# Planned slack ahead of the transposes of softmax and 1/rms, and the output projections in three parts instead of two

## The chip, the cores and the metric

The kernel runs on one core of one Trainium2 chip. The time is that of the device for one execution, in microseconds (us); "the median" is that of three executions. One further execution was recorded by the hardware profiler; all durations and waits below are from it. TensorE multiplies matrices (PE in the profile, its weight loads PEld), VectorE (DVE) and ScalarE (ACT) work element by element, GpSimd (POOL) computes a few small powers, and the queue of SyncE (SP) starts the transfers between HBM and the on-chip memory SBUF. TensorE writes its results to banks of the accumulator memory PSUM.

## What is computed

Two layers of a decoder over 256 positions of width 1024, all in float32. Each layer normalizes x, projects it to 4360 columns, runs three groups of heads, and adds an output projection of their joint result to x:

```python
def hybrid_layer(x, norm_w, w_in, ..., w_out):
    h = rmsnorm(x, norm_w)
    proj = jnp.matmul(h, w_in)
    (aq, ak, av, ag, bq, bk, bv, bg, cq, ck, cv, co, cg, ci, cf) = jnp.split(proj, cuts, axis=-1)
    ya = merge_heads(moba_attention(aq, ak, av)) * silu(ag)      # 8 heads, softmax with a distance term
    yb = head_norm(retention(rotate(bq), rotate(bk), bv)) * silu(bg)   # 4 heads
    yc = head_norm(mlstm(conv(cq, ck), cv, ci, cf) * sigmoid(co)) * silu(cg)   # 4 heads
    return x + jnp.matmul(jnp.concatenate([ya, yb, yc], -1), w_out)

def reference(x, ...):
    for layer in range(2):
        x = hybrid_layer(x, ...)
    return rmsnorm(x, final_norm_w)
```

With 256 positions and blocks of 256, the block-sparse attention is plain causal attention with a distance term.

## The kernel before

x lies transposed in SBUF (`px`), so that the projections need no transposes of it. Weights come in chunks of up to 128x2112 through three `raw` buffers. Each chunk is split into two parts, `hi` (rounded by ScalarE to float32r, the type of the matmuls) and `lo` (what is left, subtracted by VectorE), with three buffers each; x is split in the same way into `xh` and `xl` (the tile `xx`), the heads' result y into `yh` and `yl`. A product is then three matmuls: hi*hi, hi*lo, lo*hi. Projections accumulate in four PSUM banks `pj`; everything else that TensorE makes (scores, transposes, attention times values) goes to four banks `mx`. A chunk's `hi` and `lo` buffers are given back once the last matmul that reads them has been placed.

The order of the instructions on every engine is set when the program is built, by the class `Sched`. Each step of work is a generator that yields one instruction at a time with an engine and an estimated cost. The scheduler keeps a planned time for each engine, and always places next the instruction that can start earliest by that plan; among equals a priority decides. An instruction of a thread may start when its own predecessor is planned to end, plus 230 ns (`LAT`) if that was on another engine. `wait(ev)` holds a thread until an event's planned time. What is placed is final: at run time each engine takes its instructions in that order and waits by semaphores where an operand isn't there. The plan's costs decide the order and nothing else.

The three places that the change touches are these. `norm(l)` computes 1/rms: sums of squares, a power on GpSimd (`G(630, ...)`, line 488), and then two transposes on TensorE (`TR`, line 285) that spread it over a row, `rrow`. The queries and keys of all groups are scaled by it. `head_a` is one head of the softmax: scores (`dots`), a maximum by VectorE into `sb`, two exponentials by ScalarE on `sb`, and three transposes of `sb` into a bank `pt`, which ScalarE copies to `et`; `pair_a` then multiplies `et` by the values `va`. The output projections are the last part of `project` for the first layer and `out_last` for the second. Both take four weight chunks (`ws_`, rows 768, 512, 0 and 256 of w_out) in two parts of two: for each PSUM bank the matmuls of both chunks of the part, then the next bank; the buffers of both come back after the last bank. In the first layer a part waits at its start for the first half of each of its chunks.

Two more helpers matter here. `evac_gate` makes the gate tiles `t` (one for each half of the positions) from the last projections, multiplies them by the heads' results `hc`, `on_b` or `on_a` on VectorE, and `y_out` transposes them on TensorE into `mx`. `head_norm` normalizes heads on VectorE, with a power on GpSimd (line 1095). In the records all VectorE work has line 259, all ScalarE work 265, matmuls 280, transposes 285 and transfers 288, because helpers issue them.

Of the kernel before, what the change touches and what calls it, by code (L numbers as in the profile page):

```python
# [12 lines left out]
AF = mybir.ActivationFunctionType  # L13
# [215 lines left out]
def trunk(ctx: ExitStack, tc: tile.TileContext, xp: bass.AP, w: bass.AP, fn: bass.AP,  # L229
# [41 lines left out]
    def G(cost, fn, after=None):  # L271
        return op("pool", cost, fn, after)
# [17 lines left out]
    def wait(ev):  # L290
        return ("wait", ev)
# [4 lines left out]
    def acq(tag):  # L296
        return ("acq", tag)


    px = sb_tile([128, P_N + KT * S], "px")  # L300
# [166 lines left out]
    def norm(l):  # L467
# [19 lines left out]
        rs = tiny(2)  # L487
        yield G(630, lambda: nc.gpsimd.tensor_tensor(rs, ms, mhalf[:, :2], op=OP.pow))  # L488
        yield wait(E("tab"))
        for b in range(2):  # L490
            yield TR(p[:, 128 + b * 128:256 + b * 128], rs[:, b:b + 1].to_broadcast([128, 128]))
# [69 lines left out]
    def project():  # L561
        for l in range(DEPTH):
# [103 lines left out]

            for part in (ws_[:2], ws_[2:]):
                at_chunk[0] = part[-1][0]
                if part[0] is ws_[2]:
                    sc.spawn(norm(l + 1), -1)  # L670
                for i, _ in part:
                    yield wait(E("w", i, 0))
                for ds_, tag in groups:
# [24 lines left out]
    def out_last(base):  # L698
# [3 lines left out]
        acc = {}  # L702
        for part in (0, 1):
            pw = ws_[2 * part:2 * part + 2]
            at_chunk[0] = pw[-1][0]
            for b in range(2):
# [3 lines left out]
                for j, (c0, c1) in enumerate(cuts):  # L710
                    if part == 0:
                        acc[b, c0] = yield acq("mx" if c0 == 768 else "pj")
# [3 lines left out]
                    for n, (i, ch) in enumerate(pw):  # L716
                        h = his[i][:, :2048].rearrange("p (r c) -> p r c", r=2)
                        lo = los[i][:, :2048].rearrange("p (r c) -> p r c", r=2)
                        for r in range(2):
                            yield wait(E("w", i, r))  # L720
                            yield wait(E("y", l, ch + r))
                            yield M(o, yh[:, ch + r, bs], h[:, r, c0:c1], part + n + r == 0, False)
                            yield M(o, yh[:, ch + r, bs], lo[:, r, c0:c1], False, False)
                            e = yield M(o, yl[:, ch + r, bs], h[:, r, c0:c1], False, part + n + r == 3)
# [126 lines left out]
    def head_a(l, g, u, hh, et, done):  # L851
# [12 lines left out]
        yield A(sb[:, 0:128], sb[:, 0:128], AF.Exp, scale=f, bias=m[:, 0:1])  # L864
        yield A(sb[:, 128:384], sb[:, 128:384], AF.Exp, scale=f, bias=m[:, 1:2])
        pt = yield acq("mx")
        for j in range(3):
            e = yield TR(pt[:, j * 128:(j + 1) * 128], sb[:, j * 128:(j + 1) * 128])
# [336 lines left out]
```

## Time and profile before

| | |
|---|---|
| median of three executions | 303.66 us (303.3 to 306.15) |
| the profiled execution | 304.55 us |
| its span, from the first instruction to the last | 302.8 us |
| TensorE busy | 293.0 us (97%), 1792 records |
| VectorE busy | 259.4 us (86%) |
| ScalarE busy | 195.2 us (64%) |
| GpSimd busy | 16.7 us (6%) |
| transfers' share of 16 DMA engines | 45.8% |
| share of the chain that ended last | PE 82%, ACT 9% |
| granted TensorE clock, mean | 0.997 |

The profiled execution took 1.75 us more than its span and 0.89 us more than the median. "Busy" is a sum over the whole program and hides stages; matmul ends are modelled, so that waits on TensorE are read from the distance between starts.

### The profile page before, as it was taken

The numbers are of one execution on the slowest core, as the hardware profiler recorded it, in microseconds if no ns is written. First come the engines' busy times: TensorE is split into PE (matmuls) and PEld (weight loads), VectorE is DVE, ScalarE is ACT, GpSimd is POOL, SyncE is SP. The second block draws the span as 40 slices with busy tenths as digits, with TensorE's granted clock in tenths as the row PEclk, the third lists the DMA queues.
The fourth block names the chain that finished last, engine by engine and source line by source line (L and its number), as shares of the span: only waits on it lengthen the run. The fifth ranks groups of instructions, "written<-read, shape, count | busy, mean of one in ns | idle before, by whom it ended". The sixth has DMA issues, their size and how long they took to land.

```text
span 302.8 us, 4794 instructions
## 1 busy us (share of the span) xinstructions
PE 293.0 (97%) x1792; PEld 258.7 (85%) x1792; DVE 259.4 (86%) x551; ACT 195.2 (64%) x339; POOL 16.7 (6%) x19
## 2 busy tenths in 40 slices
PE   8899999999999999999999999999999999999991
PEld 6798989888999888899988888988899988888881
DVE  3878999989999999766879999999999999867553
ACT  5966999699537528635666689778645264944332
POOL 5001000000002002000020000000002003000010
PEclk9999999999999999999999999999999999999998
DMA  6999446555610434841616751646540625250003
GB/s 199 378 384 359 143 153 227 192 203 197 218 63 0 149 130 139 278 141 19 261 16 259 245 181 41 238 141 202 215 141 0 218 77 179 84 210 0 0 2 139
DMA packets 9095, 48.58 MB, mean 160 GB/s; under 512 B 1008, under 2 KB 1904, under 8 KB 4080
## 3 DMA queue, kind: packets, MB, share of 16 engines
q1 hardware_dynamic: 9072, 48.28, 45.8%
q8 instruction: 14, 0.23, 0.3%
q14 instruction: 9, 0.07, 0.1%
HBM read 47.23 MB, written 1.05 MB: 159 GB/s over the span
## 4 chain that ended last, share of the span: by engine, by line
PE 82%; ACT 9%; issue 2%; DMA 2%; POOL 1%; DVE 1%; SPq 1%; POOLq 0%
PE pj L280 64%; PE mx L280 14%; ACT t L265 4%; PE mx L285 4%; ACT hi L265 3%; DMA px<-xp 2%; POOL small L488 1%; DVE lo L259 1%; ACT sb L265 1%; SPq L288 1%; ACT st L265 1%; POOL small L547 0%; ACT xx L265 0%; ACT raw L265 0%; POOLq L1201 0%
## 5 line engine op out<-in xcount | busy, mean ns | idle before, releaser
L259 DVE TENSOR_TENSOR lo<-raw,hi 128x1024 fp32r<-128x1024 f32 (+2 forms) x96 | 102.8, 1085 | 8.7 <-ACT hi L265 8.6
L280 PE MATMUL pj<-hi,xx 128*128 128x512 f32 (+1 forms) x320 | 93.1, 372 | 0.0
L265 ACT ACTIVATE hi<-raw 128x1024 fp32r<-128x1024 f32 (+2 forms) x96 | 88.4, 946 | 6.6 <-DMA raw<-w 3.3
L280 PE MATMUL pj<-xx,hi 128*128 128x512 f32 (+1 forms) x272 | 88.0, 377 | 0.8 <-ACT hi L265 0.8
L280 PE MATMUL pj<-xx,lo 128*128 128x256 f32 x240 | 69.2, 288 | 0.3 <-DVE lo L259 0.2
L280 PEld LDWEIGHTS pj<-hi,xx 128*128 128x128 f32 x320 | 57.5, 188 | 9.1
L280 PE MATMUL pj<-lo,xx 128*128 128x512 f32 (+1 forms) x160 | 59.7, 373 | 0.0
L280 PEld LDWEIGHTS pj<-xx,hi 128*128 128x128 f32 x272 | 50.1, 193 | 10.1 <-ACT hi L265 1.9
L280 PEld LDWEIGHTS pj<-xx,lo 128*128 128x128 f32 x240 | 45.9, 191 | 0.8 <-DVE lo L259 0.7
L280 PEld LDWEIGHTS pj<-lo,xx 128*128 128x128 f32 x160 | 30.1, 188 | 4.5
L265 ACT ACTIVATE t<-pj 128x256 f32<-128x256 f32 x26 | 9.8, 378 | 18.4 <-PE pj L280 18.4
L265 ACT ACTIVATE sb<-sb,small 128x128 f32<-128x128 f32 (+1 forms) x48 | 19.3, 447 | 3.2 <-DVE sb L259 2.1
L265 ACT ACTIVATE st<-t 64x512 fp32r<-64x512 f32 x26 | 16.1, 627 | 5.8 <-DVE small L259 3.2
L1095 POOL TENSOR_TENSOR small<-small,mhalf 128x8 f32<-128x8 f32 x4 | 7.5, 1868 | 181.6 <-DVE small L259 181.6
L280 PE MATMUL pj<-yh,lo 128*128 128x256 f32 x56 | 16.0, 286 | 0.0
L280 PE MATMUL pj<-yh,hi 128*128 128x256 f32 x56 | 15.9, 284 | 0.0
L280 PE MATMUL pj<-yl,hi 128*128 128x256 f32 x56 | 15.8, 283 | 0.0
L280 PE MATMUL mx<-st,st 128*128 128x128 f32 (+1 forms) x64 | 15.0, 269 | 0.0
L265 ACT ACTIVATE t<-pj,small 128x512 f32<-128x512 f32 (+1 forms) x12 | 7.3, 610 | 9.2 <-PE pj L280 9.2
L265 ACT ACTIVATE t<-t 32x512 f32<-32x512 f32 (+1 forms) x20 | 12.5, 629 | 0.3
L280 PEld LDWEIGHTS mx<-st,st 128*128 128x128 f32 x64 | 12.1, 189 | 0.4
L259 DVE TENSOR_TENSOR t<-pj,t 128x256 f32<-128x256 f32 x26 | 10.9, 418 | 1.8 <-ACT t L265 1.5
(151 smaller groups left out, 481.5 us busy)
## 6 DMA issues: line engine op xcount, KB each, us to landing
raw<-w SPq DMA_DIRECT2D x37, 1024.0 KB, 4.8
raw<-w SPq DMA_DIRECT2D x2, 1056.0 KB, 5.4
raw<-w SPq DMA_DIRECT2D x6, 256.0 KB, 5.4
raw<-w SPq DMA_DIRECT2D x2, 512.0 KB, 6.2
tb<-tab SPq DMA_DIRECT2D x1, 960.0 KB, 9.7
px<-xp SPq DMA_DIRECT2D x3, 256.0 KB, 5.2
tb<-tab SPq DMA_DIRECT2D x1, 514.0 KB, 7.1
raw<-w SPq DMA_DIRECT2D x4, 128.0 KB, 2.9
```

What stands on the lines that cost most here:

```text
L259: return op("dve", cost, lambda: getattr(nc.vector, name)(out, *a, **k), after)
L265: return op("act", cost, lambda: nc.scalar.activation(out, in_, func, **k), after)
L280: return op("pe", cost, lambda: nc.tensor.matmul(out, a, b, start=start, stop=stop, skip_group_check=True), after)
L285: return op("pe", 110.0, lambda: nc.tensor.transpose(out, in_, idn))
L288: return op("sp", cost, lambda: nc.sync.dma_start(out, in_))
L488: yield G(630, lambda: nc.gpsimd.tensor_tensor(rs, ms, mhalf[:, :2], op=OP.pow))
L1095: yield G(1600, lambda: nc.gpsimd.tensor_tensor(vs, vs, mhalf[:, :8], op=OP.pow))
```

## The change

A new helper `pause(t)` holds a thread until the planned time t. In `norm` the two transposes of 1/rms now start, by the plan, no earlier than 500 ns after the end of the power as other engines see it (the value that `yield` gives back, the end plus 230 ns); in `head_a` the three transposes no earlier than 400 ns after that of the second exponential, with the bank `pt` taken ahead of the pause. No instruction is added for this: other work that is ready takes the place in between. The output projections of both layers now go over the banks three times: with the first chunk, with the second, and with the third and fourth together. In the first layer the wait at a part's start for all its chunks is gone (each matmul still waits for its own half). The number of matmuls and the flags of first and last accumulation are the same in effect.

```diff
+    def pause(t):
+
+        ev = Event()
+        ev.time = t
+        return wait(ev)
...
-        yield G(630, lambda: nc.gpsimd.tensor_tensor(rs, ms, mhalf[:, :2], op=OP.pow))
+        e = yield G(630, lambda: nc.gpsimd.tensor_tensor(rs, ms, mhalf[:, :2], op=OP.pow))
         yield wait(E("tab"))
+        yield pause(e + 500)
         for b in range(2):
             yield TR(p[:, 128 + b * 128:256 + b * 128], rs[:, b:b + 1].to_broadcast([128, 128]))
...
-            for part in (ws_[:2], ws_[2:]):
+            for part in (ws_[:1], ws_[1:2], ws_[2:]):
                 at_chunk[0] = part[-1][0]
                 if part[0] is ws_[2]:
                     sc.spawn(norm(l + 1), -1)
-                for i, _ in part:
-                    yield wait(E("w", i, 0))
                 for ds_, tag in groups:
...
-        for part in (0, 1):
-            pw = ws_[2 * part:2 * part + 2]
+        for pw in (ws_[:1], ws_[1:2], ws_[2:]):
+            part = len(pw) - 1
             at_chunk[0] = pw[-1][0]
...
-                    if part == 0:
+                    if pw[0] is ws_[0]:
                         acc[b, c0] = yield acq("mx" if c0 == 768 else "pj")
...
-                            yield M(o, yh[:, ch + r, bs], h[:, r, c0:c1], part + n + r == 0, False)
+                            yield M(o, yh[:, ch + r, bs], h[:, r, c0:c1], pw[0] is ws_[0] and r == 0, False)
                             yield M(o, yh[:, ch + r, bs], lo[:, r, c0:c1], False, False)
                             e = yield M(o, yl[:, ch + r, bs], h[:, r, c0:c1], False, part + n + r == 3)
...
-        yield A(sb[:, 128:384], sb[:, 128:384], AF.Exp, scale=f, bias=m[:, 1:2])
+        e = yield A(sb[:, 128:384], sb[:, 128:384], AF.Exp, scale=f, bias=m[:, 1:2])
         pt = yield acq("mx")
+        yield pause(e + 400)
         for j in range(3):
             e = yield TR(pt[:, j * 128:(j + 1) * 128], sb[:, j * 128:(j + 1) * 128])
```

Because every later choice of the scheduler depends on the earlier ones, instructions move all over the program. Transfers and GpSimd keep their order, and two copies of x for the last sum move from VectorE to ScalarE. Three places follow.

On TensorE, in the first layer, at the transposes of 1/rms (`small` is the tile of small values; `pj_120` and `pj_121` are the banks of the projection that runs meanwhile, `xx` the split x, `hi_90` and `lo_93` the weights):

```order
 L280 MATMUL pj_121<-xx,lo_93 128x256
 L280 MATMUL pj_120<-xx,hi_90 128x512
+L280 MATMUL pj_120<-xx,lo_93 128x256
+L280 MATMUL pj_121<-xx,hi_90 128x512
+L280 MATMUL pj_121<-xx,lo_93 128x256
 L285 MATMUL mx_122<-tb,small 128x128 x2
-L280 MATMUL pj_120<-xx,lo_93 128x256
-L280 MATMUL pj_121<-xx,hi_90 128x512
-L280 MATMUL pj_121<-xx,lo_93 128x256
```

Three matmuls of the projection now stand ahead of the two transposes. At the first softmax of each layer the transposes of `sb` move back in the same way.

On TensorE, in the second layer, where the second four heads' softmax meets the first gates (`t` are gate tiles, `sb_111` to `sb_113` the heads' exponentials). Before:

```order
L280 MATMUL pj_120<-hi_88,xx 128x512
L280 MATMUL pj_121<-hi_88,xx 128x512
L285 MATMUL mx_123<-tb,sb_111 128x128 x3
L280 MATMUL pj_121<-lo_91,xx 128x512
L280 MATMUL pj_121<-hi_88,xx 128x512
L285 MATMUL mx_125<-tb,sb_112 128x128 x3
L280 MATMUL pj_120<-hi_88,xx 128x512
L285 MATMUL mx_122<-tb,t_95 128x128
L285 MATMUL mx_122<-tb,t_97 128x128
```

The same place now:

```order
L280 MATMUL pj_120<-hi_88,xx 128x512
L280 MATMUL pj_121<-hi_88,xx 128x512
L285 MATMUL mx_122<-tb,t_99 128x128
L285 MATMUL mx_122<-tb,t_97 128x128
L285 MATMUL mx_122<-tb,t_99 128x128
L285 MATMUL mx_122<-tb,t_97 128x128
L285 MATMUL mx_125<-tb,sb_111 128x128 x3
L285 MATMUL mx_124<-tb,sb_112 128x128 x3
L280 MATMUL pj_121<-lo_91,xx 128x512
```

The four gate transposes, which stood behind those of two heads and three matmuls, now stand ahead of all of these.

On VectorE, in the same stretch, somewhat earlier (`zu` and `zd` are the rests of the split keys, `small` 128x8 are the sums of `head_norm`, whose power GpSimd takes between the TENSOR_SCALAR and the later TENSOR_TENSOR on it; ISA is the maximum of a head's scores). Before:

```order
L259 TENSOR_TENSOR zu_108<-t_96,st_100 64x512
L259 TENSOR_REDUCE small<-t_99 128x8
L259 TENSOR_TENSOR zd_110<-t_96,st_101 64x512
L259 TENSOR_SCALAR small<-small 128x8
L259 TENSOR_TENSOR lo_92<-raw_86,hi_89 128x1024
L259 ISA sb_111,small<-mx_123,tb 128x128
L259 ISA small 128x1
L259 TENSOR_TENSOR lo_92<-raw_86,hi_89 128x1024
L259 TENSOR_TENSOR small<-small 128x8
```

The same place now:

```order
L259 TENSOR_TENSOR lo_92<-raw_86,hi_89 128x1024
L259 TENSOR_REDUCE small<-t_96 128x8
L259 CAST st_101<-t_94 64x512
L259 TENSOR_SCALAR small<-small 128x8
L259 TENSOR_TENSOR zu_108<-t_94,st_100 64x512
L259 TENSOR_TENSOR zd_110<-t_94,st_101 64x512
L259 TENSOR_TENSOR lo_92<-raw_86,hi_89 128x1024
L259 TENSOR_TENSOR small<-small 128x8
L259 ISA sb_111,small<-mx_125,tb 128x128
```

The first of the maxima comes after both halves of `lo` and after the product with the power, and between the power's input and its use stand three instructions that read two SBUF tiles each.

## Rows read from the trace of the kernel before

**Rows 1.** The page's first part: busy us (share of span) xinstructions.

```profile
PE 293.0 (97%) x1792; PEld 258.7 (85%) x1792; DVE 259.4 (86%) x551; ACT 195.2 (64%) x339; POOL 16.7 (6%) x19
```

**Rows 2.** Timeline of PE at both transposes of 1/rms: start, duration, what [idle before].

```profile
23.00 0.39 PE L280 MATMUL pj<-xx,hi 128*128 128x512 f32 x1
23.62 0.43 PE L285 MATMUL mx<-tb,small 128*128 128x128 f32 x2 [0.23 <-POOL small L488]
...
157.75 0.27 PE L280 MATMUL pj<-xx,lo 128*128 128x256 f32 x1
158.12 0.43 PE L285 MATMUL mx<-tb,small 128*128 128x128 f32 x2
```

**Rows 3.** Timeline of PE at four heads' softmax transposes.

```profile
43.77 0.27 PE L285 MATMUL mx<-tb,sb 128*128 128x128 f32 x1
...
44.54 0.48 PE L280 MATMUL pj<-xx,hi 128*128 128x512 f32 x1
...
181.31 0.78 PE L285 MATMUL mx<-tb,sb 128*128 128x128 f32 x3
181.85 0.36 PE L280 MATMUL pj<-xx,lo 128*128 128x256 f32 x1
...
185.53 0.40 PE L280 MATMUL pj<-xx,hi 128*128 128x512 f32 x1
185.76 0.27 PE L285 MATMUL mx<-tb,sb 128*128 128x128 f32 x1
...
186.64 0.36 PE L280 MATMUL pj<-xx,lo 128*128 128x256 f32 x1
...
259.11 0.49 PE L285 MATMUL mx<-tb,sb 128*128 128x128 f32 x3
259.35 0.48 PE L280 MATMUL pj<-lo,xx 128*128 128x512 f32 x1
```

**Rows 4.** Timeline of PE in both output projections.

```profile
141.83 0.28 PE L280 MATMUL pj<-yh,hi 128*128 128x256 f32 x1
141.95 0.28 PE L280 MATMUL pj<-yl,hi 128*128 128x256 f32 x1
142.22 0.39 PE L280 MATMUL pj<-yh,lo 128*128 128x256 f32 x1
...
287.06 0.40 PE L280 MATMUL pj<-hi,yh 128*128 128x512 f32 x1
287.61 0.50 PE L280 MATMUL pj<-lo,yh 128*128 128x512 f32 x1
287.95 0.40 PE L280 MATMUL pj<-hi,yl 128*128 128x512 f32 x1
```

**Rows 5.** Stretch 159 to 260.5: length, busy PE, PEld, DVE, ACT, POOL; PEclk; DMA.

```profile
159.00:260.50 101.50, 101.02 (x598) 88.42 (x597) 98.39 (x215) 67.61 (x113) 4.18 (x2) 1.00 0.48 166
```

**Rows 6.** Timeline of VectorE: its two real gaps from 159 to 229 us.

```profile
177.60 0.42 DVE L259 TENSOR_TENSOR t<-pj,t 128x256 f32<-128x256 f32 x1 [0.58 <-ACT t L265]
...
213.31 1.23 DVE L259 TENSOR_TENSOR lo<-raw,hi 128x1024 fp32r<-128x1024 f32 x1 [0.41 <-ACT hi L265]
```

**Rows 7.** Timeline of weight loads near 229 us.

```profile
229.19 0.19 PEld L280 LDWEIGHTS mx<-ub,sel 128*128 128x128 f32 x1 [0.22 <-DVE on_a L259]
```

**Rows 8.** Timeline of VectorE, second layer, ahead of the gates' transposes.

```profile
252.22 1.22 DVE L259 TENSOR_TENSOR lo<-raw,hi 128x1024 fp32r<-128x1024 f32 x1
...
254.97 0.17 DVE L259 TENSOR_TENSOR small<-small 128x8 f32<-128x8 f32 x1 [0.18 <-POOL small L1095]
...
259.14 0.75 DVE L259 TENSOR_TENSOR t<-t,hc 128x256 f32<-128x256 f32 x2
```

**Rows 9.** Timeline of PE at the gates' first transposes.

```profile
260.46 0.49 PE L285 MATMUL mx<-tb,t 128*128 128x128 f32 x3
```

**Rows 10.** Timeline of GpSimd: both powers of the second layer's `head_norm`.

```profile
230.82 1.64 POOL L1095 TENSOR_TENSOR small<-small,mhalf 128x8 f32<-128x8 f32 x1 [72.75 <-DVE small L259]
252.39 2.54 POOL L1095 TENSOR_TENSOR small<-small,mhalf 128x8 f32<-128x8 f32 x1 [19.93 <-DVE small L259]
```

## The prediction

> **What bounds the kernel now.** I read the page's busy times first, then the distances between starts on TensorE, then what ended each distance that is longer than usual, and last how full the other engines are in the stretches where that happens. TensorE is busy 293.0 of 302.8 us and VectorE 259.4 [rows 1]. So a transpose that stands too early in TensorE's order holds up the matmuls behind it, and those set the end. What such a wait costs is the distance from one start to the next less what the same pair usually takes: 0.12 us behind a matmul of 256 columns (141.83 to 141.95) [rows 4], 0.23 us behind one of 512 (185.53 to 185.76) [rows 3], and 0.24 us from the first of three transposes to the matmul behind them (259.11 to 259.35) [rows 3].
>
> The second thing to see is that TensorE isn't alone. From 159 to 260.5 us, which is most of the second layer, VectorE is busy 98.39 of 101.50 us [rows 5]. Its two real gaps there before 229 us are 0.58 us at 177, for a copy by ScalarE, and 0.41 us at 213, for a weight half that ScalarE hadn't rounded yet [rows 6]. Near 229 us TensorE waits 0.22 us for a bank that VectorE has just emptied [rows 7]. Here both engines run side by side, and time taken off one alone is not time off the kernel.
>
> **The change part by part.**
>
> The transposes of 1/rms. In the first layer the start comes 0.62 us after that of the matmul of 512 columns ahead of it [rows 2], 0.39 us more than usual; in the second 0.37 us after one of 256 columns, 0.25 us more. The order now puts three matmuls ahead of the first pair (256, 512 and 256 columns: 0.12 + 0.23 + 0.12 = 0.47 us), which covers 0.39; in the second layer the same kind of step covers 0.25. Both waits go, 0.64 us. What is late next is the copy to `rrow` and all that is scaled by it; the pair itself comes 0.1 to 0.3 us later than now, which VectorE takes up in the second layer in its gap of 0.58 us [rows 6], so I cost that at nothing; without that cover it would cost those 0.1 to 0.3 us.
>
> The softmax transposes. Three heads wait: 43.77 to 44.54 is 0.77 us against 0.24, so 0.53; 181.31 to 181.85 gives 0.54 - 0.24 = 0.30; 185.76 to 186.64 gives 0.88 - 0.24 = 0.64 [rows 3]. Together 1.47 us. All other heads have their exponentials in time, and for them the pause buys nothing. The 400 ns are planned time, and ScalarE lies behind its plan when it is crowded, but the matmuls put ahead (three in the first layer, 0.58 us; more in the second) are longer than the waits of 0.53 and 0.30, and about as long as that of 0.64. I take all of it as gone from these places. The price is that `et`, and so attention times values, comes later by as much; those products have other matmuls ahead of them in the order and nobody else queued behind, so nothing is added.
>
> The output projections. The third and fourth chunks' halves could only be split once both earlier chunks were given back. The waits for `lo` are 0.27 - 0.12 = 0.15 us at 141.95, and 0.55 - 0.23 = 0.32 plus 0.34 - 0.23 = 0.11 for the matmul behind it at 287.06 [rows 4]. With the first chunk taken singly its buffers come back half a part earlier (one chunk is 18 matmuls of 512 and 12 of 256 columns in the second layer: 18 x 0.23 + 12 x 0.12 = 5.6 us), and the split of one chunk is 2.4 us of VectorE (two halves of 1.22 [rows 8]). So 0.15 + 0.43 = 0.58 us goes. It adds no matmul and no copy. The wait for all chunks of a part that is dropped in the first layer cost planned time alone.
>
> So 0.64 + 1.47 + 0.58 = 2.69 us of waits can go: 0.39 + 0.53 + 0.15 = 1.07 in the first layer's work, 0.25 + 0.30 + 0.64 = 1.19 between 158 and 187 us, and 0.43 at the end.
>
> How much of it stays. The first layer's 1.07 stays: VectorE has idle time for ScalarE and TensorE there. The last 0.43 stays too, since behind 262 us VectorE is idle again. The 1.19 is different. If TensorE comes 1.19 us early to the bank at 229 us, VectorE must have come early as well, and it can only do so by closing its gaps. The first (0.58, at 177 us) lies ahead of both softmax waits, so only the 0.25 us of 1/rms can be drawn from it; the second gives at most 0.41. That is at most 0.66, and at least nothing, if the reordered work fills the gaps. I take 0.55, near the upper end, because both gaps end on ScalarE, which in turn waits for TensorE there. So 0.64 of the 1.19 is given back at 229 us.
>
> Where a wait appears. The gates' first transposes of the second layer stood at 260.46 us [rows 9]. Two of the three sets of softmax transposes and three matmuls are now behind them: 260.46 - 259.11 = 1.35 us earlier. Their operands are the products with `hc` on VectorE, two of them in 0.75 us from 259.14, so done at 259.89 [rows 8]. The second transpose of the pair would now start at 259.22, 0.67 us ahead of that. VectorE has about the same work ahead of these products as before, so the wait is 0.67 if it moves no part earlier; I take 0.5, since the order brings the products a little forward, with 0 and 0.67 as ends. Behind it TensorE's whole queue stands, since these matmuls were its work.
>
> The sum: 1.07 + 0.55 + 0.43 - 0.5 = 1.55 us. Against the profiled execution that is 304.55 - 1.55 = 303.0; it lay 0.89 us above the median, and the same 1.55 off the median gives 303.66 - 1.55 = **302.1 us**. The tail behind the last matmul isn't touched.
>
> **The rivals.**
>
> All waits go and none comes: VectorE moves up with TensorE, because its order changes too and some of its instructions come ahead of their old places. Then 303.66 - 2.69 = 301.0. For it speaks that VectorE waits for ScalarE and ScalarE for TensorE at both gaps; against it that VectorE's total hardly changes and 98.39 of 101.50 us leave little to close.
>
> The pauses don't do what they say: where ScalarE is behind its plan, the exponentials are late by more than the matmuls put ahead, so that half of the transposes' waits stay. The first layer then gives 0.46 + 0.15, the second 0.28, the end 0.43, less 0.5 at the gates: 0.82 us, so 302.8. For it speaks that the largest wait, 0.64, is in a stretch where ScalarE hasn't a gap; against it that the plan leaves out nothing in the other three.
>
> Slower, through VectorE and GpSimd ahead of the gates: the power of the second `head_norm` took 2.54 us at 252.39, the other 1.64 [rows 10]. The long one began while VectorE subtracted two SBUF tiles (252.22 to 253.44 [rows 8]) and ended 1.5 us after that subtraction's end; the short one lay beside work that reads PSUM. VectorE waited 0.18 us for it, since a further subtraction stood between. Now three instructions with two SBUF inputs follow the power's input back to back, and its user stands right behind them. If the power gets in only behind the third, VectorE waits 1.5 us, the maxima and the products for the gates are late by as much, and TensorE's wait at the gates is 0.5 + 1.5 = 2.0 us. With none of the 1.19 kept this is 1.07 + 0.43 - 2.0 = -0.5, so 304.2; it is slower than before once the wait at the gates is over 1.5. Against it: between two of those instructions the power may get in, as it did ahead of the second subtraction. The Trainium skill (SBUF — State Buffer, "Who interferes with whom") says that a VectorE instruction with two SBUF inputs and a GpSimd instruction that reads SBUF exclude each other for the length of the one that came first; the two powers' times agree with it, and by it this rival needs GpSimd to lose all three turns.
>
> **How the numbers follow.** The forecast has 0.48, all waits gone 0.17, pauses that do half 0.15, the slower case 0.13, and 0.07 is left for waits that the reordering makes elsewhere, on either side. The range goes from 300.6 (301.0 less 0.4, by which the lowest of the three executions lies below their median) to 304.2, the slower case. About 1% (3.0 us) is what a measurement of this kernel can tell from no change. Faster by that means below 300.6: a little of the second case and of the rest, 0.08. Slower means above 306.7, which only unforeseen waits or far more at the gates would give: 0.05. Within it 0.87.
>
> **What the changed profile would show.** Right: at the first layer's 1/rms and first softmax no distance on TensorE over 0.3 us; no wait for `lo` in either output projection; a wait of some tenths for VectorE near 228 us and one at the gates' first transposes, with a DVE releaser; VectorE's busy time from 159 to 260 within 1 us of before. Wrong: a wait for `sb` left at the second layer's first heads (the pauses are too short), no wait at 228 and the gates (VectorE had more room than I saw), a power over 2.5 us with VectorE idle behind it (the slower case), or any new wait on TensorE above 0.5 us elsewhere, for a `hi` or `lo` half above all, since those move with every reordering.

## The result, and the profile after

The changed kernel took **301.55 us** (median of nine executions, 300.95 to 303.24), the kernel before 303.66 (nine executions): 0.9921 of it, with a 95% interval of 0.9903 to 0.9939, so 1.9 to 2.9 us less. The forecast was 302.1. The profiled execution took 301.41 us with a span of 299.6, against 304.55 and 302.8.

Two executions of one kernel differ mostly in the head, the first 20 us with the first transfers. So three stretches are compared below, all read from starts on TensorE. The **head** ends at the first of the matmuls that sum the squares (`mx<-ones,t`); the **first layer** reaches from there to the same matmul of the second layer; the **second layer** from there to the last matmul. Behind it lie 6.34 us in both kernels.

| stretch, us | before | after | difference |
|---|---|---|---|
| head | 21.16 | 20.69 | -0.47 |
| first layer (155.69 - 21.16) | 134.53 | 133.13 | -1.40 |
| second layer (296.43 - 155.69) | 140.74 | 139.45 | -1.29 |

The changed kernel's first line of the page, and the line of its chain of waits by engine:

```profile
PE 291.0 (97%) x1792; PEld 258.2 (86%) x1792; DVE 257.7 (86%) x549; ACT 196.6 (66%) x341; POOL 15.3 (5%) x19
...
PE 91%; DVE 2%; issue 2%; ACT 1%; DMA 1%; SPq 1%; POOL 0%; POOLq 0%
```

TensorE's share of the chain rose from 82% to 91%, ScalarE's fell from 9% to 1%. The timeline of TensorE shows where (start, duration, what, with the ends of the stretches):

```profile
20.69 0.50 PE L280 MATMUL mx<-ones,t 128*128 128x1 f32 x4
...
23.10 0.28 PE L280 MATMUL pj<-xx,lo 128*128 128x256 f32 x1
23.22 0.38 PE L285 MATMUL mx<-tb,small 128*128 128x128 f32 x2
...
43.32 0.49 PE L285 MATMUL mx<-tb,sb 128*128 128x128 f32 x3
43.57 0.36 PE L280 MATMUL pj<-xx,lo 128*128 128x256 f32 x1
...
153.82 0.50 PE L280 MATMUL mx<-ones,t 128*128 128x1 f32 x4
...
156.35 0.39 PE L280 MATMUL pj<-xx,hi 128*128 128x512 f32 x1
156.58 0.38 PE L285 MATMUL mx<-tb,small 128*128 128x128 f32 x2
...
184.07 0.49 PE L285 MATMUL mx<-tb,sb 128*128 128x128 f32 x3
184.32 0.36 PE L280 MATMUL pj<-xx,lo 128*128 128x256 f32 x1
...
255.65 0.62 PE L280 MATMUL pj<-hi,xx 128*128 128x512 f32 x2
256.11 0.27 PE L285 MATMUL mx<-tb,t 128*128 128x128 f32 x1
256.56 0.55 PE L285 MATMUL mx<-tb,t 128*128 128x128 f32 x3 [0.18 <-DVE t L259]
...
293.27 0.28 PE L280 MATMUL mx<-hi,yl 128*128 128x256 f32 x1
```

Both transposes of 1/rms start 0.12 and 0.23 us behind the matmul ahead of them, the usual distances, where [rows 2] showed 0.62 and 0.37. Three softmax transposes take 0.25 us to the next matmul, where [rows 3] showed up to 0.88; so do those at 181.38 and 186.50. In both output projections no distance is longer than usual any more [rows 4]. One wait is new, at the gates [rows 9]: from 256.11 to 256.56, 0.45 us between two transposes that usually stand 0.11 apart (0.34 us), with VectorE's product `t` as releaser.

Where the prediction had a second new wait, near 228 us, there is none. Of the weight load's wait of 0.22 us in [rows 7] the matmuls had felt 0.17: in the kernel before it is 0.58 us from 228.89 to 229.47, where 0.23 and 0.18 are usual (227.90 to 228.08 for the same kind of matmul without a wait):

```profile
228.89 0.40 PE L280 MATMUL pj<-xx,hi 128*128 128x512 f32 x1
229.19 0.45 PE L280 MATMUL mx<-ub,sel 128*128 128x384 f32 x1
229.47 0.28 PE L280 MATMUL pj<-xx,lo 128*128 128x256 f32 x1
```

In the changed kernel three such matmuls follow the one ahead of them after the usual 0.23 us and take 0.59 us together:

```profile
225.26 0.39 PE L280 MATMUL pj<-xx,hi 128*128 128x512 f32 x1
225.49 0.75 PE L280 MATMUL mx<-ub,sel 128*128 128x384 f32 x3
226.08 0.28 PE L280 MATMUL pj<-xx,lo 128*128 128x256 f32 x1
```

VectorE has come with TensorE. These are windows from the sums of squares to the end of the `on_a` product that empties this bank (length, then busy time and count of PE, PEld, DVE, ACT, POOL), of the kernel before:

```profile
155.69:229.14 73.45, 72.87 (x437) 63.57 (x435) 69.51 (x137) 52.35 (x84) 1.61 (x1) 1.00 0.51 173
```

and of the changed kernel:

```profile
153.82:225.75 71.93, 71.93 (x435) 63.27 (x433) 68.81 (x138) 53.04 (x85) 1.60 (x1) 1.00 0.51 177
```

The stretch got 1.52 us shorter. VectorE's idle time in it fell from 3.94 to 3.12 us (0.82), its busy time by 0.70. Its instructions there are the same but for one: a rounding of `st` of 0.42 us now comes behind `on_a`, and a product of 0.15 us on `small` ahead of it. The last wait of VectorE in the stretch is the one for ScalarE's `hi` at 213.31 us in [rows 6]; here it is this one:

```profile
210.43 1.23 DVE L259 TENSOR_TENSOR lo<-raw,hi 128x1024 fp32r<-128x1024 f32 x1 [0.15 <-ACT hi L265]
```

From there to the end of `on_a` VectorE works, in both kernels, without a gap of more than 0.04 us. The `lo` stands 57.62 us behind the sums of squares before and 56.61 now, which is 1.01 of the 1.52 us; the run behind it takes 15.32 us instead of 15.83, which is the other 0.51. In the window of [rows 5], from 159 to 260.5 us, VectorE is busy 99.26 us instead of 98.39.

### The profile page after: what moved, and what is told of

The parts are those of the page before. It is cut to its first block, busy times and chain, and to the rows that moved or that the text cites. A ratio compares the mean times of both kernels' runs of the same rounds, so it can differ in the third digit from the quotient of the medians.

```text
span 299.6 us, 4795 instructions
## 1 busy us (share of the span) xinstructions
PE 291.0 (97%) x1792; PEld 258.2 (86%) x1792; DVE 257.7 (86%) x549; ACT 196.6 (66%) x341; POOL 15.3 (5%) x19
## 4 chain that ended last, share of the span: by engine, by line
PE 91%; DVE 2%; issue 2%; ACT 1%; DMA 1%; SPq 1%; POOL 0%; POOLq 0%
PE pj L280 71%; PE mx L280 15%; PE mx L285 4%; DMA px<-xp 1%; SPq L288 1%; DVE sb L259 1%; DVE t L259 1%; ACT t L265 0%; ACT hi L265 0%; POOL small L554 0%; ACT xx L265 0%; ACT raw L265 0%; POOLq L1207 0%; DVE raw L259 0%; DVE hc L259 0%
## 5 line engine op out<-in xcount | busy, mean ns | idle before, releaser
L280 PE MATMUL pj<-hi,xx 128*128 128x512 f32 (+1 forms) x320 | 94.4, 374 | 0.0
L1101 POOL TENSOR_TENSOR small<-small,mhalf 128x8 f32<-128x8 f32 x4 | 6.9, 1731 | 181.7 <-DVE small L259 181.7
```

The costliest lines, as they stand in the source:

```text
L280: return op("pe", cost, lambda: nc.tensor.matmul(out, a, b, start=start, stop=stop, skip_group_check=True), after)
L1101: yield G(1600, lambda: nc.gpsimd.tensor_tensor(vs, vs, mhalf[:, :8], op=OP.pow))
```

## The experiments

Two theories stood against each other after the result. **Waits add up**: the time falls by what TensorE waited for at the places of the change, in both layers, and VectorE follows, since its order is replaced too. **VectorE holds the second layer**, as predicted: of the second layer's gain 0.55 us stays at most. A third was that the gain is an accident of the new order. Each batch of four ran beside the kernel before on its chip; the ratio is to those runs.

| kernel | median, us | before beside it | ratio (95%) | head | first layer | second layer |
|---|---|---|---|---|---|---|
| before | 303.66 | | | 21.16 | 134.53 | 140.74 |
| after | 301.55 | 303.66 | 0.9921 (0.9903 to 0.9939) | 20.69 | 133.13 | 139.45 |
| e1 both pauses | 303.54 | 304.49 | 0.9958 (0.9929 to 0.9987) | 22.97 | 133.44 | 139.89 |
| e2 three parts | 303.30 | 304.49 | 0.9962 (0.9928 to 0.9995) | 21.54 | 133.81 | 139.91 |
| e3 pauses, first layer | 303.58 | 304.49 | 0.9977 (0.9950 to 1.0004) | 21.08 | 133.43 | 140.74 |
| e4 pauses, second layer | 304.18 | 304.49 | 0.9992 (0.9962 to 1.0021) | 23.10 | 134.41 | 139.98 |
| e5 after again | 301.43 | 304.13 | 0.9906 (0.9872 to 0.9939) | 20.58 | 133.10 | 139.44 |
| e6 VectorE +1.38 | 303.65 | 304.13 | 0.9982 (0.9952 to 1.0012) | 21.33 | 133.07 | 140.91 |
| e7 VectorE -3.2 | 301.83 | 304.13 | 0.9915 (0.9886 to 0.9945) | 21.82 | 133.15 | 139.31 |
| e8 gates' pause | 301.88 | 304.13 | 0.9905 (0.9871 to 0.9939) | 20.90 | 133.12 | 139.43 |
| e9 softmax 100 ns | 302.82 | 303.78 | 0.9942 (0.9914 to 0.9971) | 19.98 | 134.16 | 139.53 |
| e10 softmax 1200 ns | 305.69 | 303.78 | 1.0072 (1.0045 to 1.0098) | 22.60 | 136.61 | 139.98 |
| e11 before, VectorE -3.2 | 303.90 | 303.78 | 1.0013 (0.9982 to 1.0044) | 21.69 | 134.30 | 140.71 |
| e12 no pause at 1/rms | 301.99 | 303.78 | 0.9927 (0.9898 to 0.9956) | 20.70 | 133.22 | 139.71 |

Medians include the head, and the intervals are some 0.5 to 1.0 us to either side; the stretches, from one profiled execution of each kernel, are finer. In the five kernels that change nothing in the changed kernel's first layer or only its gates' order (after, e5 to e8) the first layer lies between 133.07 and 133.15. In the three that have the first layer of the kernel before (before, e4, e11) it lies between 134.30 and 134.53, so that a gain in the first layer is sure to some 0.2 us only. In the three that have its second layer (before, e3, e11) that lies between 140.71 and 140.74.

### The parts by themselves (e1 to e4)

e1 is the kernel before with both pauses, e2 the change without them:

```diff
# e1: the kernel before, and
+        yield pause(e + 500)
...
+        yield pause(e + 400)
# e2: the changed kernel, and
-        yield pause(e + 500)
...
-        yield pause(e + 400)
```

> Both pauses, with the output projections as before. If the time is the sum of TensorE's waits and VectorE follows: the pauses' 0.92 in the first layer and 1.19 in the second go, less 0.35 at the gates, whose transposes stand here as in the changed kernel: 1.76 us, so 301.9, with the waits for lo still at the output projections (0.15 and 0.43). If the nearly full VectorE gives the second layer's gain back, as predicted: 0.92 + 0.55 - 0.5 = 0.97, so 302.7, with a wait of some 0.6 on TensorE near 228 us. If what counts is where the reordering happens to put things: no relation to either number.

> Only the output projections in three parts, no pauses. Sum of waits, and lockstep with VectorE alike: 0.15 + 0.43 = 0.58 us, so 303.1, with all waits of the transposes still there and none for lo in the output projections. If the parts don't add up by places: anything from 302.5 to 304.

e3 and e4 are e1 with both pauses in one layer alone:

```diff
+        if l == 0:
+            yield pause(e + 500)
...
+        if l == 0:
+            yield pause(e + 400)
# e4: if l == 1
```

> Both pauses in the first layer alone, old output projections. Sum of waits, and lockstep alike: 0.39 + 0.53 = 0.92 us, so 302.7; the second layer's waits at its 1/rms and softmax transposes (1.19 together) are still there, or have moved if the second layer's order differs.

> Both pauses in the second layer alone, old output projections; the gates' transposes stand behind three heads' here, so no wait is due there. Sum of waits with VectorE following: 1.19 us, so 302.5, and no wait near 228. Lockstep, as predicted: 0.55 kept, 303.1, with 0.6 us of waits on TensorE for VectorE between 187 and 230 us.

The whole times can't tell 0.97 from 1.76 us: e1 is 0.9958, 1.3 us less with an interval of 0.4 to 2.2. The stretches can. The second layer is 0.85 us shorter in e1 and 0.76 in e4, with the wait at the gates in both, against 0.84 (1.19 - 0.35) by the sum of waits and 0.05 (0.55 - 0.5) by the prediction; in e3 it is unchanged. e4 was expected to be free of the wait at the gates, wrongly. In the first layer the pauses give 1.10 us in e3 and 1.09 in e1, against 0.92 (0.87 and 0.86 from the 134.30 of e11). Parts that repeat by stretch in this way speak against an accident. That theory isn't out altogether, though: with another length of the same pause the order brings waits of its own (e9, e10).

The three parts alone give 0.83 us in the second layer and 0.72 in the first, against 0.43 and 0.15; not all of this is theirs. From the first output matmul to the second sums of squares e2 takes 28.14 us (155.35 - 127.21), the kernel before 28.40 (155.69 - 127.29), so 0.26 less; from the second layer's first output matmul to its last 24.67 (295.26 - 270.59) instead of 25.19 (296.43 - 271.24), 0.52 less. All kernels with two parts take 28.38 to 28.40 us there in the first layer and 25.14 to 25.19 in the second; all with three parts take 28.13 or 28.14 (but for e10, which waits there for other things) and 24.66 to 24.69. Each gain is some 0.1 us over the wait that was read; in the first layer the matmul behind the late one [rows 4] had been late as well. Of the rest, 0.39 us is the first layer's wait at 1/rms, which isn't there in e2, as shown next. And 0.28 us lies in the second layer's first 25 us, in which TensorE's order is the same as before; the last section comes to it.

The profile of e2 shows that the first layer's wait at 1/rms need not be there without a pause. Its power on GpSimd and the subtraction beside it on VectorE:

```profile
22.39 0.71 POOL L494 TENSOR_TENSOR small<-small,mhalf 128x2 f32<-128x2 f32 x1 [17.24 <-DVE small L259]
...
23.06 1.23 DVE L259 TENSOR_TENSOR lo<-raw,hi 128x1024 fp32r<-128x1024 f32 x1 [0.82 <-ACT hi L265]
```

and the same two in the kernel before:

```profile
22.01 1.56 POOL L488 TENSOR_TENSOR small<-small,mhalf 128x2 f32<-128x2 f32 x1 [16.87 <-DVE small L259]
...
21.78 1.23 DVE L259 TENSOR_TENSOR lo<-raw,hi 128x1024 fp32r<-128x1024 f32 x1
```

Before, the subtraction stood 0.23 us ahead of the power and the power ended 0.56 us after it. In e2 ScalarE's rounding came later, the power was alone and took 0.71 us, and the transposes found their operand. The changed kernel's profiled execution had the short power too.

### Does VectorE hold the second layer? (e5, e6, e7, e11)

e5 is the changed kernel once more, beside e6 to e8.

> The changed kernel once more, on the chip of the next three, as their base. If the first layer's wait at 1/rms is a meeting with the transfers of the head, the stretch from the first sum of squares on TensorE to the second, and from there to the end, repeat within 0.2 us (133.1 and 139.5), and only the head before them differs.

The stretches repeat to 0.03 us.

e6 gives VectorE 1.38 us more work in the second layer and e7 takes 3.2 us from it, without a change in the plan; e11 is e7's edit on the kernel before:

```diff
-                t = yield V("tensor_tensor", lo[:, a:b], raws[i][:, a:b], h[:, a:b].bitcast(F32),
+                o = V("tensor_tensor", lo[:, a:b], raws[i][:, a:b], h[:, a:b].bitcast(F32),
                             op=OP.subtract, after=ts_[j])
# e6
+                if j and i in (NW + 5, NW + 7):
+                    fn = o[1][2]
+
+                    def both(fn=fn, d=lo[:, a:a + 512], r=raws[i][:, a:a + 512], q=h[:, a:a + 512].bitcast(F32)):
+                        nc.vector.tensor_tensor(d, r, q, op=OP.subtract)
+                        return fn()
+                    o = ("op", (*o[1][:2], both, o[1][3]))
# e7, e11
+                if j and NW + 4 <= i <= NW + 9:
+                    def half(d=lo[:, a:a + 512], r=raws[i][:, a:a + 512], q=h[:, a:a + 512].bitcast(F32)):
+                        return nc.vector.tensor_tensor(d, r, q, op=OP.subtract)
+                    o = ("op", (*o[1][:2], half, o[1][3]))
+                t = yield o
```

> The changed kernel with two more instructions on VectorE of 0.69 us each in the second layer (half a subtraction done twice, 173 and 188 us), 1.38 us, the plan unchanged, TensorE's order too. If VectorE sets the second layer's pace together with TensorE (the prediction's reason), the time rises by 1.2 to 1.4 us: waits on TensorE for VectorE of that sum between 174 and 230. If TensorE sets it and VectorE only follows, with idle time enough to take it up (1.6 us from 157 to 226), by under 0.4 us.

> The changed kernel with 3.2 us less work on VectorE in the second layer (six halves of lo are subtracted over 512 columns instead of 1024, so that half of them is left out), plan and TensorE's order unchanged. If VectorE sets the pace there, the second layer gets shorter by 1 us or more. If TensorE sets it: only the wait at the gates goes, 0.35 us at most, and VectorE has some 3 us more idle time.

> The kernel before with 3.2 us less work on VectorE in the second layer (half of six halves of lo left out), TensorE's order unchanged. If the softmax waits of the second layer (0.30 and 0.64) come from VectorE running behind the plan, they go: the second layer is 0.9 us shorter (139.8 instead of 140.74). If they are the plan's own (ScalarE's exponentials take longer than the scheduler allows), they stay: less than 0.3 shorter, by the wait for VectorE at 229 us.

e6 cost 1.47 us in the second layer (140.91 - 139.44), all of the added work, as was expected of a VectorE that sets the pace. By the distances on TensorE 1.10 us of it stand at three places behind the added instructions, which ran at 174.4 and 190.5 us: 0.18 at 182.0, 0.30 at 184.9 and 0.62 at 215.1. TensorE's weight loads wait for the exponentials again, and its transposes for the small gate values:

```profile
182.25 0.20 PEld L285 LDWEIGHTS mx<-tb,sb 128*128 128x128 f32 x2 [0.27 <-ACT sb L265]
185.29 0.20 PEld L285 LDWEIGHTS mx<-tb,sb 128*128 128x128 f32 x2 [0.49 <-ACT sb L265]
```

```profile
215.85 0.38 PE L285 MATMUL mx<-tb,small 128*4 128x128 f32 x2 [0.46 <-DVE small L259]
```

e7 gained 0.13 us. In the window that answers to the changed kernel's 157 to 225.8, VectorE is now busy 64.29 of 68.80 us instead of 67.07, and TensorE 68.80 of 68.80 as before; the wait at the gates, which was expected to go, is still there:

```profile
158.15:226.95 68.80, 68.80 (x414) 60.52 (x413) 64.29 (x134) 51.69 (x83) 0.00 (x0) 1.00 0.54 183
```

```profile
257.57 0.55 PE L285 MATMUL mx<-tb,t 128*128 128x128 f32 x3 [0.18 <-DVE t L259]
```

So after the change TensorE sets the second layer, and VectorE has no slack at the two places where work was added: 1.38 us more shows whole, 3.2 us less almost not at all. The idle time of 3.12 us in that stretch of the changed kernel was no slack for them; 2.21 us of it are five gaps of 0.15 to 0.72 us that end on TensorE or ScalarE. What e7 doesn't tell is what VectorE's work later in the layer costs. Its six shorter subtractions all end before 201 us, and at 211.41 VectorE again waits for ScalarE's `hi`, for 0.40 us, 56.44 us behind the sums of squares (56.61 in the changed kernel), so that nearly all that it had gained is lost by there, long before the gates.

e11 asks the same of the kernel before, and its second layer stayed (140.71 against 140.74). The softmax waits are still there, the second of them for `sb`, though two of the six shorter subtractions lie ahead of them; VectorE's load had not made them. And the wait at 229 us, on which the prediction had rested most, is there to the hundredth. Weight load, VectorE ahead of it, and TensorE at the second softmax wait, in e11:

```profile
229.51 0.19 PEld L280 LDWEIGHTS mx<-ub,sel 128*128 128x128 f32 x1 [0.22 <-DVE on_a L259]
```

```profile
213.62 1.23 DVE L259 TENSOR_TENSOR lo<-raw,hi 128x1024 fp32r<-128x1024 f32 x1 [0.40 <-ACT hi L265]
...
227.90 1.22 DVE L259 TENSOR_TENSOR lo<-raw,hi 128x1024 fp32r<-128x1024 f32 x1
229.03 0.42 DVE L259 TENSOR_TENSOR on_a<-mx,small 128x256 f32<-128x256 f32 x1
```

```profile
186.77 0.44 PE L285 MATMUL mx<-tb,sb 128*128 128x128 f32 x2 [0.42 <-ACT sb L265]
```

The bank waits for `on_a`, and `on_a` stands behind a `lo` of 1.22 us in VectorE's order. In the changed order the instruction ahead of `on_a` is another, of 0.69 us, and TensorE loses nothing there. But e11 doesn't settle what makes the wait. Its shorter subtractions all end before 203 us, and at 213.62 us VectorE waits for ScalarE's `hi`, 57.63 us behind the sums of squares, where the kernel before has 57.62: what it had gained is lost by there. From there to `on_a` it works without a gap, at the same instructions. So VectorE's load ahead of 213 us doesn't make the wait at 229; whether its load behind it does, or the one `lo`, no run tells apart.

### The wait at the gates (e8)

```diff
-            sc.spawn(y_out(l, y, j, halves[j][1], done := Event()), 1, e)
+            sc.spawn(y_out(l, y, j, halves[j][1], done := Event(), e), 1, e)
...
-    def y_out(l, y, j, ch, done):
+    def y_out(l, y, j, ch, done, e):
         q = yield acq("mx")
+        yield pause(e + 600)
```

> The changed kernel with a third pause, of 600 ns, ahead of the transposes of the gates: in the second layer three transposes of a head and a matmul of 512 columns now stand ahead of them (0.47 us). By the sum of TensorE's waits the wait of 0.35 us at the gates goes and nothing else moves: 0.35 us less than the changed kernel. If the wait only moves to the next instruction that needs VectorE (the transposes' slack was 0.06 us), 0.0 to 0.1 less.

The gates' transposes no longer wait: four take 0.44 us, from 256.79 to 257.23. But the second layer is 139.43 us, 0.01 less, because a weight load now waits 0.39 us for the copy `et` by ScalarE, two microseconds on:

```profile
256.79 0.60 PE L285 MATMUL mx<-tb,t 128*128 128x128 f32 x4
257.23 0.82 PE L285 MATMUL mx<-tb,sb 128*128 128x128 f32 x6
```

```profile
259.11 1.08 PEld L280 LDWEIGHTS mx<-va,et 128*128 128x128 f32 x9 [0.39 <-ACT et L265]
```

By the distance between starts TensorE loses 0.31 us there. The wait moved, as the second of the two expectations had it, though to an instruction that needs ScalarE, not VectorE. None of the kernels shown here is faster than the changed one.

### How long a pause (e9, e10), and the pause at 1/rms (e12)

```diff
# e9                              # e10
-        yield pause(e + 400)     -        yield pause(e + 400)
+        yield pause(e + 100)     +        yield pause(e + 1200)
# e12
-        yield pause(e + 500)
```

> The changed kernel with a softmax pause of 100 ns instead of 400. One matmul of 512 columns stands ahead of the first head's transposes instead of three matmuls, and the second layer's heads stand some four rows earlier. If each wait is what the matmuls put ahead don't cover: in the first layer 0.53 - 0.23 = 0.30 us comes back (stretch 133.4 instead of 133.1), in the second some 0.6 of 0.94. If the transposes only had to leave their first place by anything: nothing comes back.

> The changed kernel with a softmax pause of 1200 ns. If slack past what a wait needs costs nothing (other work takes the place): both layers' stretches as in the changed kernel within 0.1 us; the gates' transposes stand behind two heads' here, and the wait there goes or moves, as with the pause at the gates. If the bank that is held through the pause, or later attention products, hold others up: waits on TensorE or VectorE, and 0.5 us or more on top.

> The changed kernel without the pause at 1/rms. By the sum of waits: 0.25 us comes back in the second layer (139.7 instead of 139.44), and in the first 0.39 if TensorE is through with the head's matmuls as early as in the changed kernel (20.6 us), nothing if it is half a microsecond later. Where VectorE sets the second layer's pace: nothing there.

e9: with 100 ns the first head's transposes take 0.53 us again where 0.24 is usual, 0.29 as expected:

```profile
42.26 0.77 PE L285 MATMUL mx<-tb,sb 128*128 128x128 f32 x3
42.79 0.36 PE L280 MATMUL pj<-xx,lo 128*128 128x256 f32 x1
```

The first layer lost 1.06 us, though: other waits for VectorE appeared with the new order, among them 0.28 us at 108.4 and 0.2 for a weight load at 79.6; where the rest was lost was not traced. The second lost only 0.09 instead of 0.6: of its softmax waits 0.32 us is left at 184, and in exchange the one at the gates is gone.

e10: three times the pause isn't free, it makes the kernel slower than before. The first layer is 3.5 us longer than with 400 ns. The largest single wait comes from GpSimd. Its power took 4.03 us; VectorE waited for it, and TensorE later for VectorE:

```profile
93.37 4.03 POOL L1101 TENSOR_TENSOR small<-small,mhalf 128x8 f32<-128x8 f32 x1 [68.36 <-DVE small L259]
```

```profile
93.54 2.34 DVE L259 TENSOR_TENSOR lo<-raw,hi 128x1024 fp32r<-128x1024 f32 x2
95.81 0.41 DVE L259 TENSOR_TENSOR t<-pj,t 128x256 f32<-128x256 f32 x1
97.43 0.17 DVE L259 TENSOR_TENSOR small<-small 128x8 f32<-128x8 f32 x1 [1.21 <-POOL small L1101]
```

```profile
100.74 0.38 PE L280 MATMUL mx<-st,st 128*128 128x256 f32 x1 [0.80 <-DVE sb L259]
...
131.05 0.38 PE L280 MATMUL pj<-yh,hi 128*128 128x256 f32 x1 [0.57 <-ACT yh L265]
131.80 0.39 PE L280 MATMUL pj<-yl,hi 128*128 128x256 f32 x1 [0.37 <-DVE yl L259]
```

The two last rows are the other price: the heads' results come late at the output projection, where TensorE waits for them. By the distances between starts the four waits in the first layer come to 0.95, 0.50, 0.73 and 0.63 us (at 99.6, 115.5, 130.2 and 131.1), 2.8 of the 3.5. The held bank named in the expectation shows no wait of its own in the first layer. The second layer, 0.53 us longer than the changed kernel's, has one of 0.66 us, at the gates' transposes:

```profile
262.57 0.63 PE L280 MATMUL pj<-hi,xx 128*128 128x512 f32 x2
263.68 0.55 PE L285 MATMUL mx<-tb,t 128*128 128x128 f32 x3 [0.49 <-ACT et L265]
```

ScalarE's copy `et` released them. They don't read `et`; they write to one of the four banks `mx`, and `et` is copied out of one. So this is a wait for a bank that a head of the softmax had held, as the second expectation had it.

e12: in the second layer 0.25 us came back at the transposes as expected (0.36 us from 155.99 to 156.35, where 0.11 is usual). At the second head's transposes 0.46 us came too, and the wait at the gates went: 0.25 + 0.46 - 0.34 = 0.37, measured 0.27. In the first layer 0.09 came back instead of 0.39, which is hardly more than the stretch scatters by (133.07 to 133.15): the power was the short one, and the transposes start without a wait.

```profile
21.55 0.70 POOL L494 TENSOR_TENSOR small<-small,mhalf 128x2 f32<-128x2 f32 x1 [16.41 <-DVE small L259]
```

## Why the prediction was right or wrong

The forecast of 302.1 us was 0.55 us above the median. Its sum of 1.55 us stands against 2.69 us in the two layers of the profiled executions (1.40 + 1.29), and 1.9 to 2.9 us by the ratio. The difference of the two profiled executions, 3.14 us, has 0.47 us of head in it, which the change doesn't touch. The chance of 0.87 "within it" belongs to 300.6 to 306.7 us, since 0.08 and 0.05 are what is given for times outside these; the range up to 304.2 has no chance of its own.

- **TensorE's waits set the time.** Right. Where parts of the change were put in alone, the stretches got shorter by about the distances that were too long in them, and elsewhere by nearly nothing but for 0.28 us in e2. The share of the chain, which rose to 91%, is no proof of it: e8 takes the same time in both layers with PE at 82% and DVE at 9%.
- **The transposes' waits go, 0.64 and 1.47 us.** Right in the places and close in the sums: 0.87 to 1.10 us in the first layer (e3) for 0.92, and in the second 0.76 to 0.85 net of the gates' 0.34, so 1.10 to 1.19, for 1.19. Only the reason of the first layer's 0.39 was incomplete: TensorE waits there when the power on GpSimd takes 1.56 us instead of 0.71. With the short power the same pause is worth 0.09 at most (e12).
- **The output projections, 0.15 and 0.43 us.** Right, and somewhat small: 0.26 and 0.52 (e2).
- **"So 0.64 of the 1.19 is given back at 229 us."** This step failed. Nothing was given back (e4: 0.76 us with the gates' wait in it, where the prediction's step leaves 0.05). VectorE was through with `on_a` 1.52 us earlier after the sums of squares, where the prediction allowed 0.66 at most. What was wrong in it is "it can only do so by closing its gaps". The gaps gave 0.82 us, from all the idle time of 3.94 us and not only from the two gaps of [rows 6], 0.99 us. The other 0.70 is less time busy ahead of this point: the order of VectorE changed along with TensorE's, and one rounding of 0.42 us moved behind `on_a`; the rest of the 0.70 was not traced. The prediction knew that VectorE's order changes and took its work ahead of `on_a` as fixed all the same. The rival "all waits go and none comes" had named this, and was right on VectorE. That the new order would do so wasn't worked out by either. The prediction's other fact was sound where it was tried: VectorE has no room for more at 174 and 190 us (e6). Whether the wait of [rows 7] was a sign of an engine at its limit stays open: less work ahead of 203 us leaves it at 0.22 (e11), and less work behind 213 us was not tried.
- **A new wait at the gates, 0.5 us, with VectorE as releaser.** Right in place and cause; the term was mis-sized, 0.34 us measured. That nothing but it stands between the kernel and more speed would be wrong: without it the next wait, for `et`, takes its place (e8).
- **Slower, through VectorE and GpSimd.** It didn't come about at the gates: there the power took 2.00 us, and VectorE, at its three instructions until 251.37 us, didn't wait for it. The mechanism is real and its price was near: in e10 another order put two subtractions of two SBUF tiles behind a power's input, and VectorE waited 1.21 us (1.5 was assumed).
- **The pauses do half.** Wrong at 400 and 500 ns; it is what e9 shows of 100 ns at the first head.

The errors add up: 0.64 us not given back, 0.33 more from the first layer (of which some 0.2 may be scatter), 0.09 from the last projection and 0.16 from the gates are 1.22 us, against the 1.14 by which the sum was short. They all lie on one side, so no error hid another. But that the new order brought one new wait and not more was luck as far as the prediction goes: it had 0.07 for waits elsewhere and no way to tell, and e9 and e10, with another length of the same pause, lost 1.1 and 3.5 us in the first layer.

## What to carry to other kernels

When a program sets the order ahead of time, a transpose that stands too early on the fullest engine can cost its wait in full, as those here did, and a little planned slack, about as long as the wait, bought that back; three times as much delayed what comes later and cost 4 us. A second engine that is 97% busy doesn't by itself hold up the first: where a change gives it a new order too, its work ahead of a given point can shrink along with its gaps. To test whether its load makes a wait, take the work out between its own last wait and the place in question; what is taken out ahead of that is lost again by that wait, as nearly all of it was in e7 and e11. And where one wait goes, look for the next in line a few instructions on before building its removal.

## What the runs showed of the hardware

A power of GpSimd on a tile of 128x2 took 0.71 us alone and 1.56 us when VectorE began a subtraction of two SBUF tiles 0.23 us ahead of it. On a tile of 128x8 it took 4.03 us where VectorE began two such subtractions in a row just behind it (e10), and 1.63 to 1.65 undisturbed; VectorE ran the two in 2.34 us without a break. The Trainium skill (SBUF — State Buffer, "Who interferes with whom") says that a VectorE instruction with two SBUF inputs contends with a GpSimd instruction that reads SBUF. These times agree with it. In e10 the power ended 1.52 us after the second subtraction, so that by these times GpSimd got no turn between the two.

It isn't always so. At the changed kernel's gates the power began beside the first of three such instructions; it ended 1.49 us after that one (249.39), while the other two went on at their usual 0.69 and 1.23 us:

```profile
248.88 2.00 POOL L1101 TENSOR_TENSOR small<-small,mhalf 128x8 f32<-128x8 f32 x1 [20.36 <-DVE small L259]
```

And in e9 a subtraction of two SBUF tiles began 0.97 us into a power, and neither took longer than alone:

```profile
232.19 1.64 POOL L1101 TENSOR_TENSOR small<-small,mhalf 128x8 f32<-128x8 f32 x1 [75.67 <-DVE small L259]
```

```profile
233.16 1.22 DVE L259 TENSOR_TENSOR lo<-raw,hi 128x1024 fp32r<-128x1024 f32 x1
```

So in these runs a power was held by what VectorE had under way near its start, and a power under way held no VectorE instruction. In e9 the two didn't contend, where that sentence of the Trainium skill would have it that they do. Why the power got in behind the first instruction at the gates and only behind the second in e10 was not tested; the records differ in that 0.03 us lie between those two at the gates, and in e10 the second begins at 94.68 before the first ends at 94.75.

The head took between 19.98 and 23.10 us, longest in e1, e4 and e10. In these three alone the clock granted to TensorE fell to 0.50 of full speed, 1.2 instead of 2.4 GHz; in e4 from about 12 to 15 us, after TensorE had waited 1.69 us for the first weights at 9.8 us and 0.26 us at 11.7. In e1 and e10 the first of these waits was 1.12 and 1.23 us. In e11 it was 1.58, with 0.25 behind it, and the clock stayed at 1.00; so the length of the wait alone doesn't tell them apart, and what does was not studied. The window from 12 to 14 us (the third value from the end is the granted clock), in e4:

```profile
12.00:14.00 2.00, 2.00 (x11) 2.00 (x11) 2.00 (x6) 2.00 (x7) 0.00 (x0) 0.50 1.05 418
```

and in e11:

```profile
12.00:14.00 2.00, 2.00 (x18) 2.00 (x18) 2.00 (x7) 2.00 (x7) 0.00 (x0) 1.00 1.05 416
```

Single executions of one kernel scatter by more than the change, from 303.08 to 307.24 us for the kernel before beside e1 to e4, in part through this: in e4, five of the twelve executions had a mean clock of 0.990 to 0.992, and these are the five above 305 us.

Pairs of a 512- and a 256-column matmul ran at slightly different distances in different executions: with TensorE's order unchanged, e2's second layer reached its first softmax transposes 25.34 us after the sums of squares (180.69 - 155.35), the kernel before 25.62 (181.31 - 155.69). The difference grew evenly from about 3 to 18 us of that stretch and not behind it, and both have the same wait of 0.25 us at 1/rms; e3 and e11, with the same order there, took 25.63 us like the kernel before. The cause stays open.
